# Float32r gate products, paired entry blocks and a split collection in a two-block transformer kernel

## The chip, the cores and the metric

The kernel runs on one NeuronCore of one Trainium2 chip. The metric is device time of one execution in microseconds (us). A core has TensorE (matrix products, PE in the profile, its weight loads PEld), VectorE (DVE), ScalarE (ACT), GpSimd (POOL) and SyncE (SP, which issues nearly all DMAs). Each engine works through its own queue in order; semaphores tie the queues together.

## The reference

One token block of 256 tokens with 1024 features goes through two transformer blocks, all in float32. The first has a mixer (retention and differential attention), then a product-key expert layer; the second has two layers of a gated short convolution or block attention, memory cross-attention and a SwiGLU. The expert layer is where most of the time lies:

```python
q = (hb @ w_query).reshape(t, PEER_HEADS, 2, PEER_HALF)
s = jnp.einsum('thpc,hpnc->thpn', q, sub_keys)
...
best, pos = lax.top_k(cand, PEER_TOPK)
experts = jnp.take_along_axis(cand_idx, pos, axis=-1)
gate = jax.nn.softmax(best, axis=-1)
act = jax.nn.gelu(jnp.einsum('thkd,td->thk', expert_u[experts], hb), approximate=False)
return jnp.einsum('thk,thkd->td', gate * act, expert_v[experts])
...
z = c_gate * u                     # short convolution: 3 taps over z, then
return (b_gate * conv) @ w_out     # gated by b_gate
```

Each token picks 16 experts in each of 8 heads, out of 128 x 128.

## The kernel before, in words

Activations lie transposed: features on the 128 partitions in 8 chunks, 256 tokens along the free axis. Precision comes from splitting: a weight tile `raw` (128x1024) is loaded by SP, rounded to float32r by ACT (`whi`, L118), and the rest is subtracted by DVE or POOL (`wlo`, L122, by `lo_plan`: "v" is DVE, "p" POOL). A block (`block`, L156; `mm3`, L134) is then 24 matmuls of 128x128 weights with 256 tokens: eight chunks each of whi·h_hi, wlo·h_hi and whi·h_lo. Its order is pass by pass, or, with `late`, chunk by chunk. There are three buffers of `raw` and `whi`, two of `wlo`. Large stages are dense rows of such blocks.

The expert layer (`peer`, L712) doesn't gather. It computes all 128x128 experts for all tokens: `slots` (128 partitions x 128 chunks x 256 tokens, 128 KB per partition) takes gelu(U·h2), is multiplied with a dense gate, and is multiplied with V.
- Entry: h2 is made chunk by chunk by DVE and ACT after a norm; 16 query blocks with `scores` behind each; `route` (DVE) picks the top 16 of each token, some steps after each block.
- U stage: 64 pairs of blocks (`peer_u`). From pair 16 on, gate groups stand between the blocks (`groups`). A group (`group`, L884) is four tokens: for each, `hot` builds two one-hot matrices on DVE (ohA: one comparison for two tokens; ohB: comparison times gate, one for each token) from `iota`, which lies in PSUM, and TensorE multiplies them in fp32, which gives the token's 128x128 gate. DVE multiplies it into the chunks that are done (L896, strided by tokens), ACT copies it to the chunks that are not (L898). For a finished token the later pairs are multiplied with the gate by DVE (L928).
- V stage: 128 chunks; ACT and DVE split `slots[:, c]` in two halves (`acth`, `actl`), twelve matmuls of 512 columns (`product`, L952). `mod_rest` loads and sums the last modulation weights beside the first of them. At the end `collect` copies, transposes and adds the output; the copies lie in the first slots.

Then comes the second block: `conv_mixer` (its `hook` loads the stored memory keys and values at block 1), `mem_attn`, `swiglu`, `moba`. A generator `filler` puts blocks of the memory's keys and values into waits, at places listed in `PLACES`; `track` sums squares for the next norm, adding on POOL (in the convolution's entry on DVE).

Order within each engine's queue is fixed at compile time by the framework's scheduler (program order as priority, by modelled times). Two readers of one PSUM bank of a tile are put one after the other.

Of the kernel before, what the change touches and what calls it, by code (L numbers as in the profile page):

```python
# [25 lines left out]
P = 128  # L26
T = 256
D = 1024
KC = 8
# [11 lines left out]
PLACES = {0: 1, 3: 1, 5: 2, 6: 1, 10: 1, 12: 1, 's': 2, 'h': 4, 'g': 10, 'n': 1, ('g', 0): 1, 'v': 4, ('d', 1): 1, ('o', 0): 3, ('o', 2): 1, ('o', 3): 1, ('o', 4): 1, ('o', 5): 4, ('o', 7): 10, ('c', 1): 1, ('c', 3): 1, ('c', 5): 1, 'ce': 1, 'm0': 1, 'mq0': 1, 'me0': 1, 'f0': 1, 'b': 2, 'bk': 1, 'bq': 1, ('mh0', 2): 1, ('bh', 0): 1, ('bh', 5): 1, ('bh', 7): 1}  # L41
# [15 lines left out]
CADD = 'vector'  # L57
MIXLO = 'v'
RETLO = 'v'
AHEAD = 3  # L60
# [11 lines left out]
class Build:  # L72
    def __init__(self, ctx, tc, io):
# [8 lines left out]
        self.adder = self.nc.gpsimd  # L82
# [51 lines left out]
    def mm3(self, out, pairs, first=True, last=True, late=False):  # L134
# [4 lines left out]
        if late:  # L139
            order.sort(key=lambda si: (si[1], si[0]))  # L140
# [15 lines left out]
    def block(self, out, src, x, cols=slice(None), lo=None, late=False, w=None):  # L156

        wh, wl = w or self.weight(src, lo)
        self.mm3(out, [(wh[:, k * P:(k + 1) * P], wl[:, k * P:(k + 1) * P],
                        x[0][:, k, cols], x[1][:, k, cols]) for k in range(KC)], late=late)  # L160

# [33 lines left out]
    def rstd(self, pool, sums, n, tag, shape=(P, T), bufs=1, a=None, y=None, tables=False, behind=None):  # L195
# [7 lines left out]
        log = nc.scalar.activation(y, a, AF.Ln)  # L203
# [79 lines left out]
    def constants(self):  # L283
# [6 lines left out]
        nc.vector.memset(self.ones, 1.0)  # L290
        self.x = c.tile([P, KC, T], F32, name="x")
# [10 lines left out]

    def mod_start(self, pool):
# [4 lines left out]
        warm = self.psum([P, P], "aux")  # L308
        for _ in range(WARM):
            nc.tensor.matmul(warm, self.ones, self.ones, start=True, stop=True)  # L310
# [136 lines left out]
    def mixer(self):  # L447
        nc, io, tc = self.nc, self.io, self.tc
        with ExitStack() as ctx:
# [7 lines left out]
            with ExitStack() as c1:  # L457
# [31 lines left out]
                for b in range(2):  # L489
                    for i in range(2):  # L490
                        self.block(gates[b][:, i], io["w_in_t"][12 + 2 * b + i], h, cols=X, late=b == i == 0)
                    self.at(("g", b))
# [158 lines left out]
            self.fill(20)  # L651

# [59 lines left out]
    def peer(self):  # L712
        nc, io = self.nc, self.io
        with ExitStack() as ctx:
            self.banks(ctx, "peer")
            big = self.pool(ctx, "slots")
            pool = self.pool(ctx, "peer")
            slots = big.tile([P, NCH, T], F32, name="slots")
            h = self.placed(pool, "h2h", 48), self.placed(pool, "h2l", 48)
# [16 lines left out]
            selT = gpool.tile([P, 3, T], F32, name="selT")  # L736
# [104 lines left out]
            def turn():  # L841

                for tt in range(2):
# [4 lines left out]
                    nc.scalar.copy(selT[:, :, cols], tr)  # L848
# [7 lines left out]
            ahead = query(0)  # L856
            for j in range(16):
                self.lo_plan = QPLAN[j // 4]
                q = ahead
                if j < 15:  # L860
                    ahead = query(j + 1)
# [6 lines left out]
            NG = T // TG  # L868

            def hot(g):  # L870


                for j in range(2):
                    A = gpool.tile([P, 2, P], F32, name="ohA", tag="ohA", bufs=HOT)
                    Bt = gpool.tile([P, 2, P], F32, name="ohB", tag="ohB", bufs=HOT)
                    t = g * TG + 2 * j
                    nc.vector.tensor_tensor(A, iota[:, None, :].to_broadcast([P, 2, P]),
                                            selT[:, 1, t:t + 2, None].to_broadcast([P, 2, P]), op=OP.is_equal)
                    for i in range(2):
# [72 lines left out]
            def product(c, th, a, b, w):  # L952
                tsl = slice(th * P, th * P + P)
                for s, (x, wt) in enumerate(((a, w[0]), (b, w[0]), (a, w[1]))):
                    for dh in range(2):
# [3 lines left out]
            def collect(th):  # L959

                tsl = slice(th * P, th * P + P)
                for q in range(4):
                    e = nc.scalar.copy if th or q % 2 else nc.vector.tensor_copy
                    e(ot[:, th, q * T:(q + 1) * T], acc[th][:, q // 2, q % 2 * T:q % 2 * T + T])
                for q in range(2):
                    tr = self.psum([P, 4, P])
                    for i in range(4):
                        k = 4 * q + i
                        nc.tensor.transpose(tr[:, i], ot[:, th, k * P:(k + 1) * P], self.ident)
                    for i in range(4):  # L970
                        k = 4 * q + i
                        nc.vector.scalar_tensor_tensor(self.x[:, k, tsl], tr[:, i], gate[:, k:k + 1],
                                                       self.x[:, k, tsl], op0=OP.mult, op1=OP.add)

            gate = self.mod[:, 40:48, 0]
            ot = slots[:, 0:8, :].rearrange("p (a c) t -> p a (c t)", a=2)
            for c in range(NCH - 2):
# [7 lines left out]
            ends = [(c, chunk(c)) for c in (NCH - 2, NCH - 1)]  # L985
# [637 lines left out]
```

## Time and profile before

| | us |
|---|---|
| median of 3 runs (lowest to highest) | 1889.74 (1888.1 to 1890.78) |
| profiled execution, of which span | 1882.41, 1880.6 |
| PE busy, of the span | 1833.2 (97%) |
| DVE / ACT / POOL busy | 1313.8 / 975.1 / 453.7 |

The span runs from the first to the last instruction of one profiled execution. A busy TensorE is not TensorE at its peak: matmuls are pipelined and each record holds its latency too, so the pace is read from the distance of starts. "Idle before" names what ended an engine's wait. The stages lie about so: mixer 0 to 287 us, queries to 347, U to 762, V to 1120, second block to the end.

### The profile page before, as it was taken

To read this page: it belongs to the slowest core of one execution; us is meant where nothing else is said; L and a number is where in the kernel's file an instruction comes from. 1 tells how busy PE (TensorE), PEld (TensorE's weight loads), DVE (VectorE), ACT (ScalarE), POOL (GpSimd) and SP (SyncE) were. 2 spreads that over 40 slices of the span, in tenths; PEclk is the share of its full clock that TensorE was granted. 3 is DMA by queue.
4 is the path that set the end of the run, shared out by engine and by line. 5 is a ranking of instruction groups with operands and counts; after the bars stand their busy time and mean duration, and the time that the engine had idled before them with its cause. 6 is when DMAs were issued, how large, how long until landed. Compare 5 with 4: busy or idle time off the path is not lost.

```text
span 1880.6 us, 34809 instructions
## 1 busy us (share of the span) xinstructions
PE 1833.2 (97%) x13562; PEld 1717.2 (91%) x13562; DVE 1313.8 (70%) x2592; ACT 975.1 (52%) x1533; POOL 453.7 (24%) x254
## 2 busy tenths in 40 slices
PE   8999999999999999999999998999999999999997
PEld 6796888999999999788888878999999999999997
DVE  7879875995566676865555568777765679766654
ACT  7746335445555444445545555465554645555543
POOL 0001105787766777100000004112000111110001
PEclk9999999999999999999999999999999999999999
DMA  8763444454444444755555555544555553445553
GB/s 298 254 217 105 142 129 156 170 189 169 150 160 154 157 157 157 247 191 195 195 191 193 196 192 184 191 169 148 200 193 196 190 180 124 169 136 190 187 184 124
DMA packets 99765, 335.13 MB, mean 178 GB/s; under 512 B 12400, under 2 KB 13456, under 8 KB 99216
## 3 DMA queue, kind: packets, MB, share of 16 engines
q1 hardware_dynamic: 98160, 330.68, 51.0%
q8 instruction: 106, 1.74, 0.4%
q10 hardware_dynamic: 1440, 2.23, 0.3%
q14 instruction: 59, 0.48, 0.1%
HBM read 329.59 MB, written 3.28 MB: 177 GB/s over the span
## 4 chain that ended last, share of the span: by engine, by line
PE 87%; DVE 6%; DMA 3%; ACT 3%; issue 1%; POOL 0%; SPq 0%; DVEq 0%; ACTq 0%; POOLq 0%
PE mm L144 54%; PE pair L956 17%; PE mm L179 4%; PE pair L893 3%; PE fill L179 2%; DVE wlo L122 2%; PE fill L144 1%; PE sc L144 1%; DMA mraw<-w_mod 1%; PE aux L144 1%; DMA raw<-w_mod 1%; ACT whi L118 1%; DMA raw<-peer_v 0%; PE sc L628 0%; PE sc L554 0%
## 5 line engine op out<-in xcount | busy, mean ns | idle before, releaser
L118 ACT CAST whi<-raw 128x1024 fp32r<-128x1024 f32 x564 | 591.9, 1051 | 558.3 <-PE mm L144 280.4
L122 DVE TENSOR_TENSOR wlo<-raw,whi 128x1024 fp32r<-128x1024 f32 x420 | 526.7, 1255 | 298.7 <-PE pair L956 131.6
L122 POOL TENSOR_TENSOR wlo<-raw,whi 128x1024 fp32r<-128x1024 f32 x144 | 344.7, 2395 | 131.6 <-PE mm L144 113.6
L144 PE MATMUL mm<-hh,whi 128*128 128x256 f32 (+1 forms) x1184 | 178.2, 287 | 5.9 <-DVE ct L1248 5.1
L144 PE MATMUL mm<-hl,whi 128*128 128x256 f32 (+1 forms) x1184 | 174.5, 284 | 2.1 <-DVE hl L261 1.2
L144 PE MATMUL mm<-hh,wlo 128*128 128x256 f32 (+1 forms) x1184 | 175.9, 285 | 0.0
L144 PE MATMUL mm<-h2h,whi 128*128 128x256 f32 x1152 | 168.2, 289 | 4.1 <-ACT h2h L260 4.0
L226 POOL TENSOR_TENSOR acc<-acc,accsq 128x256 f32<-128x256 f32 x42 | 42.1, 1004 | 523.1 <-ACT accsq L224 523.1
L144 PEld LDWEIGHTS mm<-hh,whi 128*128 128x128 f32 x1184 | 155.4, 190 | 10.9 <-issue 7.6
L956 PE MATMUL pair<-whi,actl 128*128 128x512 f32 x512 | 158.6, 391 | 2.4 <-DVE actl L949 2.3
L956 PE MATMUL pair<-whi,acth 128*128 128x512 f32 x512 | 158.3, 390 | 0.3 <-ACT acth L948 0.2
L956 PE MATMUL pair<-wlo,acth 128*128 128x512 f32 x512 | 157.8, 389 | 0.7 <-DVE wlo L122 0.7
L144 PEld LDWEIGHTS mm<-hl,whi 128*128 128x128 f32 x1184 | 153.5, 189 | 5.0 <-DVE hl L261 1.7
L144 PEld LDWEIGHTS mm<-hh,wlo 128*128 128x128 f32 x1184 | 154.6, 190 | 3.5 <-issue 1.5
L144 PE MATMUL mm<-h2h,wlo 128*128 128x256 f32 x1152 | 157.5, 279 | 0.0
L144 PE MATMUL mm<-h2l,whi 128*128 128x256 f32 x1152 | 157.1, 279 | 0.0
L144 PEld LDWEIGHTS mm<-h2h,whi 128*128 128x128 f32 x1152 | 147.4, 192 | 5.0 <-ACT h2h L260 4.8
L144 PEld LDWEIGHTS mm<-h2h,wlo 128*128 128x128 f32 x1152 | 144.6, 189 | 0.0
L144 PEld LDWEIGHTS mm<-h2l,whi 128*128 128x128 f32 x1152 | 144.0, 189 | 0.0
L956 PEld LDWEIGHTS pair<-whi,actl 128*128 128x128 f32 x512 | 95.4, 188 | 24.4 <-DVE actl L949 5.0
L956 PEld LDWEIGHTS pair<-wlo,acth 128*128 128x128 f32 x512 | 96.0, 188 | 21.3 <-DVE wlo L122 1.1
L956 PEld LDWEIGHTS pair<-whi,acth 128*128 128x128 f32 x512 | 95.5, 188 | 20.9 <-ACT acth L948 1.5
(407 smaller groups left out, 3062.7 us busy)
## 6 DMA issues: line engine op xcount, KB each, us to landing
raw<-peer_u SPq DMA_DIRECT2D x128, 512.0 KB, 3.5
raw<-peer_v SPq DMA_DIRECT2D x128, 512.0 KB, 3.5
raw<-ffn_gu SPq DMA_DIRECT2D x88, 512.0 KB, 4.3
raw<-ffn_dn SPq DMA_DIRECT2D x44, 512.0 KB, 3.9
raw<-w_mod SPq DMA_DIRECT2D x64, 256.0 KB, 3.8
raw<-conv_wi SPq DMA_DIRECT2D x24, 512.0 KB, 3.5
raw<-mem_wk SPq DMA_DIRECT2D x16, 512.0 KB, 4.5
mraw<-w_mod SPq DMA_DIRECT2D x16, 512.0 KB, 6.2
```

The costliest lines, as they stand in the source:

```text
L118: self.hi_copy = nc.scalar.copy(hi, raw)
L122: (nc.vector if plan == "v" else nc.gpsimd).tensor_sub(lo, raw, hi)
L144: self.matmul = nc.tensor.matmul(out, a, b, start=first and j == 0, stop=last and j == 3 * n - 1)
L179: self.matmul = nc.tensor.matmul(outs[i // 2][:, i % 2], a[:, k, :], b[:, w], start=k == 0 and s == 0 and i % 2 == 0, stop=k == 7 and s == ...
L226: self.adder.tensor_add(self.acc, self.acc, self.last)
L893: nc.tensor.matmul(o[:, 2 * j + i], A[:, i], Bt[:, i], start=True, stop=True)
L956: nc.tensor.matmul(acc[th][:, dh], x[:, tsl], wt[:, dh * 512:dh * 512 + 512], start=c == 0 and s == 0, stop=c == NCH - 1 and s == 2)
```

## The change

1. Gates. ohA and ohB become float32r. The transposed gate is split in a float32r part (`gate_hi`) and the ratio of the rest to it; ohB holds two matrices side by side, comparison times high part by DVE and that times the ratio by ACT. A token's product is one float32r matmul of 256 columns. The group's low halves are copied out by ACT, added by DVE; the product with the done chunks goes to POOL; the others get the sum by a DVE add. Three buffers of each instead of four, two ready ahead instead of three. The weights' low halves in this stage go by "ppvp" (one in four by DVE) instead of all by POOL.
2. Entry of the queries: `twin` runs two blocks in one order, chunk by chunk; products of ones stand in the wait before. The mixer's first two gate blocks and the convolution's first two blocks (in chunk pairs) go through `twin` as well.
3. End of V: only the last chunk is special; it goes by output halves, each collected behind the next one's product, into a tile `ot` of its own; the tiles of h2 are freed before V, and the pool of V takes their place. The convolution's first weights are loaded before that.
4. Second block: the keys' loads are spread over blocks from 3 on; the convolution's gate chain, the sums of squares, the subtractions of loaded keys and rope's product go from POOL to DVE (the gate chain's scaling to ACT); two fills move back; in `moba` the query features are made beside the values, and rope reads PSUM with tables that hold the norm. The norm's logarithm reads PSUM with a bias.

```diff
-PLACES = {... ('c', 1): 1, ('c', 3): 1, ('c', 5): 1, ...}
+PLACES = {... ('c', 5): 1, ...}
+WARM_N = 12
-GPLAN = "p"
-HOT = 4
+GPLAN = "ppvp"
+HOT = 3
-HOOK = 1
+HOOK = 3
-AHEAD = 3
+AHEAD = 2
...
-        self.adder = self.nc.gpsimd
+        self.adder = self.nc.vector
...
+    def twin(self, outs, ws, x, cols=slice(None), late=1, shared=False):
+        order = sorted(((k, s, i) for k in range(KC) for s in range(3) for i in range(2)),
+                       key=lambda z: (z[0] // late, z[1], z[2], z[0]))
+        for k, s, i in order:
+            wh, wl = ws[i]
+            xh, xl = x[0][:, k, cols], x[1][:, k, cols]
+            w = (wh, wl, wh)[s][:, k * P:(k + 1) * P]
+            self.matmul = self.nc.tensor.matmul(outs[i], w, (xh, xh, xl)[s], ...)
...
-        log = nc.scalar.activation(y, a, AF.Ln)
+        log = nc.scalar.activation(y, sums, AF.Ln, scale=1.0 / n, bias=self.eps)
...
+    def warm(self, n, bank="aux"):
+        o = self.psum([P, P], bank)
+        for _ in range(n):
+            self.nc.tensor.matmul(o, self.ones, self.ones, start=True, stop=True)
...
             self.tracked_norm(pool, "nr", urgent=True, y=self.r0, a=self.acc, tables=True)
             self.fill(20)
+            self.warm(WARM_N)
...
-                    nc.scalar.copy(selT[:, :, cols], tr)
+                    nc.scalar.copy(selT[:, :, cols], tr[:, 0:2])
+                    hi, ratio = gate_hi[:, cols], gate_ratio[:, cols]
+                    nc.scalar.copy(hi.bitcast(F32R), tr[:, 2])
+                    low, inv = stats[tt][:, 0:P], stats[tt][:, P:]
+                    nc.vector.tensor_sub(low, tr[:, 2], hi)
+                    nc.vector.tensor_scalar(inv, hi, 1e-36, None, op0=OP.max)
+                    nc.vector.reciprocal(inv, inv)
+                    nc.vector.tensor_mul(ratio, low, inv)
...
-            ahead = query(0)
+            os = [self.psum([P, T]) for _ in range(2)]
+            self.twin(os, [self.weight(io["w_query"][j]) for j in range(2)], h)
...
+                    for i in range(2):
+                        nc.vector.tensor_scalar(Bt[:, i, 0], iota, selT[:, 0, t + i:t + i + 1],
+                                                gate_hi[:, t + i:t + i + 1], op0=OP.is_equal, op1=OP.mult)
+                        nc.scalar.activation(Bt[:, i, 1], Bt[:, i, 0].bitcast(F32), AF.Copy,
+                                             scale=gate_ratio[:, t + i:t + i + 1])
...
-                    for i in range(2):
-                        nc.vector.tensor_scalar(Bt[:, i], iota, selT[:, 0, t + i:t + i + 1],
-                                                selT[:, 2, t + i:t + i + 1], op0=OP.is_equal, op1=OP.mult)
...
-                o = self.psum([P, TG, P], "pair")
+                o = self.psum([P, TG, 2, P], "pair")
...
+                lo = gpool.tile([P, TG, P], F32, name="glo", tag="glo", bufs=2)
+                nc.scalar.copy(lo, o[:, :, 1])
                 sl = slots[:, :, ts].rearrange("p c t -> p t c")
                 if done:
-                    nc.vector.tensor_mul(sl[:, :, :done], o[:, :, :done], sl[:, :, :done])
+                    nc.vector.tensor_add(lo[:, :, :done], o[:, :, 0, :done], lo[:, :, :done])
+                    nc.gpsimd.tensor_mul(sl[:, :, :done], lo[:, :, :done], sl[:, :, :done])
                 if done < NCH:
-                    nc.scalar.copy(sl[:, :, done:], o[:, :, done:])
+                    nc.vector.tensor_add(sl[:, :, done:], o[:, :, 0, done:], lo[:, :, done:])
...
             gctx.close()
+            hctx.close()
             pool = self.pool(ctx, "experts")
+            ot = pool.tile([P, 2, 1024], F32, name="ot")
...
-            ends = [(c, chunk(c)) for c in (NCH - 2, NCH - 1)]
-            for c, parts in ends:
-                product(c, 0, *parts)
-            product(ends[0][0], 1, *ends[0][1])
-            collect(0)
-            product(ends[1][0], 1, *ends[1][1])
-            collect(1)
+            parts = chunk(NCH - 1)
+            if "second" in self.parts:
+                self.conv_first = self.weight(io["conv_wi"][KC])
+            waiting = None
+            for dh in range(2):
+                for th in range(2):
+                    product(NCH - 1, th, *parts, halves=(dh,))
+                    if waiting:
+                        collect(*waiting)
+                    waiting = th, dh
+            collect(*waiting)
...
-                    nc.gpsimd.tensor_sub(lo, t, hi)
+                    nc.vector.tensor_sub(lo, t, hi)
+                    yield
...
-                cu = pool.tile([P, 2, T], F32, name="cu", tag="cu", bufs=2)
-                nc.vector.tensor_mul(cu, o, r[:, None, :].to_broadcast([P, 2, T]))
-                nc.gpsimd.tensor_mul(z, cu[:, 0], cu[:, 1])
-                nc.vector.tensor_scalar(y, z, cw[:, m, 2:3], None, op0=OP.mult)
+                nc.vector.tensor_mul(z, o[:, 0], r2)
+                nc.vector.tensor_mul(z, o[:, 1], z)
+                nc.scalar.activation(y, z, AF.Copy, scale=cw[:, m, 2:3])
...
-                nc.gpsimd.tensor_mul(y, y, r)
+                nc.vector.tensor_mul(y, y, r)
...
-                if m == HOOK:
-                    hook()
+                if m >= HOOK:
+                    for _ in range(2):
+                        next(hook, None)
...
+                if m == 0:
+                    self.twin([o[:, i] for i in range(2)], [self.conv_first, self.weight(io["conv_wi"][16])], h,
+                              late=2, shared=True)
...
+            def rope(out, o):
+                t = pool.tile([P, T], F32, name="roper", tag="roper", bufs=2)
+                nc.vector.stream_shuffle(t, o, [(i + 16) % 32 for i in range(32)])
+                nc.vector.tensor_mul(out, o, cosr)
+                nc.vector.tensor_mul(t, t, sinr)
+                nc.vector.tensor_add(out, out, t)
                 return out
```

## Rows read from the trace of the kernel before

**Rows 1.** The page, the chain that ended last: share of the span by engine.
```profile
PE 87%; DVE 6%; DMA 3%; ACT 3%; issue 1%; POOL 0%; SPq 0%; DVEq 0%; ACTq 0%; POOLq 0%
```

**Rows 2.** Busy sums by stretch: us, then PE, PEld, DVE, ACT, POOL, clock, DMA.
```profile
438.00:755.00 317.00, 317.00 (x2758) 317.00 (x2757) 196.37 (x494) 158.28 (x253) 224.82 (x95) 1.00 0.45 157
...
286.00:302.00 16.00, 11.74 (x66) 10.45 (x66) 9.68 (x23) 8.32 (x15) 4.34 (x3) 0.79 0.31 107
...
1119.50:1128.00 8.50, 5.44 (x31) 4.88 (x31) 7.85 (x23) 7.73 (x21) 0.00 (x0) 0.81 0.68 224
```

**Rows 3.** The chain that ended last, in order of time: start us, us, what.
```profile
347.84 90.34 PE mm L144 x767
...
544.95 5.46 PE mm L144 x48
...
551.30 2.83 PE mm L144 x24
...
555.02 5.46 PE mm L144 x48
...
1313.58 174.10 PE mm L144 x1536
...
1687.90 180.92 PE mm L144 x1536
```

**Rows 4.** Single instructions in order of time: start us, us, engine, line, operation, tiles.
```profile
278.82 0.73 POOL L226 TENSOR_TENSOR acc<-acc,accsq 128x256 f32<-128x256 f32 x1 [0.45 <-ACT accsq L224]
...
543.89 1.06 PE L893 MATMUL pair<-ohB,ohA 128*128 128x128 f32 x8
...
544.71 1.17 PE L144 MATMUL mm<-h2h,whi 128*128 128x256 f32 x8
...
549.01 0.31 ACT L927 ACTIVATE mm<-mm 128x176 f32<-128x176 f32 x1
...
734.62 1.27 DVE L896 TENSOR_TENSOR slots<-pair,slots 128x472 f32<-128x472 f32 x1
...
738.78 0.66 DVE L928 TENSOR_TENSOR slots<-mm,slots 128x480 f32<-128x480 f32 x1 [1.59 <-ACT mm L927]
...
756.45 2.97 DVE L949 TENSOR_TENSOR actl<-slots,acth 128x256 fp32r<-128x256 f32 x2 [0.54 <-ACT acth L948]
...
756.58 2.55 POOL L122 TENSOR_TENSOR wlo<-raw,whi 128x1024 fp32r<-128x1024 f32 x1 [1.28 <-ACT acth L948]
```

**Rows 5.** Groups of instructions by line, 438 to 755 us: count, busy us, mean ns.
```profile
L122 POOL TENSOR_TENSOR wlo<-raw,whi 128x1024 fp32r<-128x1024 f32 x95 | 227.1, 2391 | 94.0 <-PE mm L144 89.2 <-ACT slots L898 2.9 <-ACT whi L118 1.8
...
L118 ACT CAST whi<-raw 128x1024 fp32r<-128x1024 f32 x94 | 98.3, 1045 | 57.6 <-PE mm L144 51.8 <-DMA raw<-peer_u 2.9 <-POOL wlo L122 2.8
...
L896 DVE TENSOR_TENSOR slots<-pair,slots 128x128 f32<-128x128 f32 (+31 forms) x64 | 56.6, 884 | 5.2 <-PE pair L893 5.2
...
L898 ACT COPY slots<-pair 128x376 f32<-128x376 f32 (+46 forms) x63 | 33.2, 527 | 41.2 <-DVE slots L896 40.9
```

**Rows 6.** Groups of instructions by line and form, whole span.
```profile
L122 DVE TENSOR_TENSOR wlo<-raw,whi 128x1024 fp32r<-128x1024 f32 x420 | 526.7, 1255 | 298.7 <-PE pair L956 131.6 <-ACT whi L118 69.6 <-PE mm L144 43.0
...
L949 DVE TENSOR_TENSOR actl<-slots,acth 128x256 fp32r<-128x256 f32 x128 | 55.7, 436 | 4.0 <-ACT acth L948 3.8
```

**Rows 7.** Single instructions of TensorE where the queries begin.
```profile
292.16 5.85 PE L144 MATMUL mm<-h2h,whi 128*128 128x256 f32 x22 [4.05 <-ACT h2h L260]
...
302.08 0.60 PE L753 MATMUL pair<-slots 128*128 128x128 f32 x4
```

**Rows 8.** Single instructions of TensorE between the experts and the convolution.
```profile
1119.02 0.62 PE L956 MATMUL pair<-wlo,acth 128*128 128x512 f32 x2
...
1123.95 0.35 PE L144 MATMUL sc<-hh,whi 128*128 128x256 f32 x1 [2.07 <-ACT hh L274]
```

**Rows 9.** Waits of TensorE: for whom, us in total, times, longest us.
```profile
PE mm L144 <- DVE ct L1248: 5.1, 1, 5.1
...
PE sc L144 <- DVE wlo L122: 3.3, 1, 3.3
```

More of the change, by code (lines that the diff above doesn't have):

```diff
@@ L160, in block @@
                         x[0][:, k, cols], x[1][:, k, cols]) for k in range(KC)], late=late)
+    def twin(self, outs, ws, x, cols=slice(None), late=1, shared=False):
[5 more added lines that the diff above has]
+            w = (wh, wl, wh)[s][:, k * P:(k + 1) * P]
+            self.matmul = self.nc.tensor.matmul(outs[i], w, (xh, xh, xl)[s],
+                                                start=k == 0 and s == 0 and not (shared and i),
+                                                stop=k == KC - 1 and s == 2, skip_group_check=True)
     def natural(self, tag, srcs, toks, done, lo=None):
@@ L307, in mod_start @@
         nc.scalar.activation(self.sc, cc, AF.Silu)
-        warm = self.psum([P, P], "aux")
-        for _ in range(WARM):
-            nc.tensor.matmul(warm, self.ones, self.ones, start=True, stop=True)
+        self.warm(WARM)
         self.sc4 = pool.tile([P, KC, 4], F32R, name="sc4")
@@ L489, in mixer @@
                 for b in range(2):
-                    for i in range(2):
-                        self.block(gates[b][:, i], io["w_in_t"][12 + 2 * b + i], h, cols=X, late=b == i == 0)
+                    if b == 0:
+                        self.twin([gates[0][:, i] for i in range(2)], [self.weight(io["w_in_t"][12 + i]) for i in range(2)],
+                                  h, cols=X, shared=True)
+                    else:
+                        for i in range(2):
+                            self.block(gates[b][:, i], io["w_in_t"][12 + 2 * b + i], h, cols=X)
                     self.at(("g", b))
@@ L950, in chunk, with product, collect @@
                 return a, b, w
-            def product(c, th, a, b, w):
+            def product(c, th, a, b, w, halves=range(2)):
                 tsl = slice(th * P, th * P + P)
                 for s, (x, wt) in enumerate(((a, w[0]), (b, w[0]), (a, w[1]))):
-                    for dh in range(2):
+                    for dh in halves:
                         nc.tensor.matmul(acc[th][:, dh], x[:, tsl], wt[:, dh * 512:dh * 512 + 512],
                                          start=c == 0 and s == 0, stop=c == NCH - 1 and s == 2)
-            def collect(th):
+            def collect(th, dh):
                 tsl = slice(th * P, th * P + P)
[L962 to L973, printed above, removed]
+                for q in (2 * dh, 2 * dh + 1):
+                    nc.scalar.copy(ot[:, th, q * T:(q + 1) * T], acc[th][:, dh, q % 2 * T:q % 2 * T + T])
+                tr = self.psum([P, 4, P])
+                for i in range(4):
+                    k = 4 * dh + i
+                    nc.tensor.transpose(tr[:, i], ot[:, th, k * P:(k + 1) * P], self.ident)
+                for i in range(4):
+                    k = 4 * dh + i
+                    nc.vector.scalar_tensor_tensor(self.x[:, k, tsl], tr[:, i], gate[:, k:k + 1],
+                                                   self.x[:, k, tsl], op0=OP.mult, op1=OP.add)
             gate = self.mod[:, 40:48, 0]
-            ot = slots[:, 0:8, :].rearrange("p (a c) t -> p a (c t)", a=2)
-            for c in range(NCH - 2):
+            for c in range(NCH - 1):
                 if c == POS:
@@ L1349, in moba @@
             hk = self.gained(pool, self.x, G_KV)
+            nc.vector.tensor_scalar(self.gains[:, G_MIX + 1], self.gains[:, G_MIX + 1], 128.0 ** -0.5, None,
+                                    op0=OP.mult)
+            hq = [self.placed(pool, "hq" + c, 40) for c in "hl"]
+            cosr, sinr = (pool.tile([P, T], F32, name=n) for n in ("cosr", "sinr"))
             v = pool.tile([P, 2, 1024], F32, name="v")
@@ L1383, in moba @@
             kT = pool.tile([P, KC, T], F32, name="k")
-            hq = [self.placed(pool, "hq" + c, 32) for c in "hl"]
             def query(hd):
-                return plain(io["moba_wq"][hd], hq, 128.0 ** -0.5)
+                return plain(io["moba_wq"][hd], hq)
             def turned(t):
```

65 lines of the change are left out of this document (38 added, 27 removed).

## The prediction

> **What bounds the kernel now.** I read the chain that ended last first: TensorE's matmuls are 87% of it, so time is won by giving TensorE less to do or by closing its waits [rows 1]. Then I cut the span at the places the change touches and took the busy sums of each stretch [rows 2]. Between 438 and 755 us (matrix U with the gate products between its blocks) TensorE never idles, while DVE is busy 196 of 317 us, ACT 158 and POOL 225: all three have room, POOL least. The two changes of stage stand out by TensorE's granted clock: 0.79 from 286 to 302 us and 0.81 from 1119.5 to 1128 us, against 1.00 inside the stage.
>
> The chain in order of time gives the price of a block (24 matmuls of 128x256 fp32r) and of a gate group [rows 3]. Two places with 1536 matmuls each took 174.1 and 180.9 us, so one matmul goes at 113.3 or 117.8 ns; the first part of U (767 in 90.34 us) went at 117.8. Nothing in the rows says why a stage falls into one cadence or the other. From 544.95 to 555.02 us there are three blocks (5.46 + 2.83 us) and two groups: (10.07 - 8.29) / 2 = 0.89 us for a group. Its four fp32 products start at 543.89 and the next block at 544.71 [rows 4]: 0.82 us of products, the rest change-over.
>
> **The sum, part by part.** It is made against the profiled execution (1882.41 us, span 1880.6 and 1.8 around it).
>
> *Gates in float32r.* Each of the 256 tokens' products turns from one fp32 product of 128 columns into one fp32r product of 256 (high and low half of the gate side by side). A 256-column fp32r matmul is what a block is made of: 0.113 to 0.118 us, four of them 0.45 to 0.47. A group falls from 0.82 to 0.46 (without the change-over) or from 0.89 to 0.46 (with it): 64 groups give -23 to -27 us. I take -26, since both neighbours are then of one kind.
>
> *What pays for it.* The other engines get more per group, in 317 - 26 = 291 us [rows 2, 4, 5].
> ACT: 158.3 us, less the copies of L898 (33.2), plus 256 small scalings at about 0.28 (a 128x176 activation took 0.31) = 72, plus 64 copies of the low half, 512 wide, at about 0.55 (half of a 1024-wide cast, 1.045) = 35: 232 us, 80%.
> DVE: 196.4, less L896 (56.6), plus the adds of the done chunks (320 elements on average, contiguous; 480 took 0.66, so 0.45) = 29, plus the adds into the slots that are not done (192 elements with a stride; 472 strided took 1.27, so 0.55) = 35, plus 24 low halves of weights that the plan "ppvp" gives it, at 1.25 [rows 6] = 30: 234 us, 80%.
> POOL: 95 low halves less 24, 71 x 2.39 = 170, plus 64 products with the slots, 320 elements on average. POOL's 256-wide sum took 0.73 alone, so 0.9 contiguous; DVE's strided product costs about twice its contiguous one per element, so up to 1.8 here. That is 228 to 285 us, 78% to 98%. The last third, with 450 elements a product, is the tight part: per three blocks (about 9.1 us) 5.4 + 2 x 1.25 to 2 x 2.5 = 7.9 to 10.4. I take 1.6 in the mean (nearest to DVE's strided row, less its low end) and +5 us of waits for TensorE, bounds 0 and +20.
>
> What is queued behind: POOL's product waits for TensorE's group, ACT's copy and DVE's add; behind it stands a low half of a weight. Two of these are buffered, and a low half is written as soon as the pass of the block before has let its buffer go, so about two blocks stand between it and its reader; a delay of some 2 us is covered. If that cover is gone, every microsecond shows on TensorE.
>
> The trace shows one thing more against the change: at 756.45 us two DVE subtractions of 0.44 each took 2.97 us while a POOL subtraction ran [rows 4, 6]. [...] In rows: each of DVE's 24 new low halves has two SBUF inputs, and may wait out a POOL instruction (2.4) or hold one up (1.25): 24 x 1.25 = 30 us more on POOL at the worst, which makes 258 to 315 of 291. It is the reason for the +20, and for rival B.
>
> *Queries.* After the norm TensorE waits 4.05 us for the first chunk of h2, then runs 22 of two queries' 48 matmuls in 5.85 us while the eight chunks arrive (0.7 us each), and begins the first scores at 302.08, 4.1 us after these 22 [rows 7]. Chunk by chunk, only the last chunk's six matmuls (0.7) and a copy of some 0.4 stand behind the last arrival: -3 (bounds 0 and -4). The twelve products of ones lie in the 4.05 us wait: 24 passes of 128 columns, twice a group's eight (0.82), are 2.5 us, at half clock 5, so 1 us past it at the worst, which is in the bound. They would keep the clock up, and I count no more for it: the entry is then paced by DVE's chunks.
>
> *U to V.* The new pool lies where h2 lay, so the first halves of the slots can't be cast before U's last matmul: a cast and an activation of ACT, about 0.5 each by the 0.31 for 176 columns: +1 (0 to +3). The stage itself stays at 12 matmuls a chunk.
>
> *V to the convolution.* The last product starts at 1119.02 and runs 0.46, the next block starts at 1123.95 [rows 8]: 4.5 us with eight transposes. [...] Now output halves are collected behind the products of the next, the first weights of the convolution are loaded before, and the first two blocks go by pairs of chunks. Of the gap about 3 us go, of the slow stretch 1.6 to 2: -5 (bounds -1 and -7).
>
> *Convolution.* Two waits, 3.3 us for a low half of weights and 5.1 for the gated product [rows 9]. The loads of memory keys move from block 1 to blocks 3 and later, two fills move back, and the gate chain loses its POOL steps (0.73 us for 256 columns, more beside DVE) [rows 4]. Against that DVE gets the subtractions of the loaded keys and the sums of squares. I take half of the two waits, -4 (bounds 0 and -7).
>
> *Rest.* 42 POOL sums of squares and 12 subtractions go to DVE, and rope's product too; the logarithm reads PSUM one DVE step sooner, but the table load stands in the same place. Gates of the mixer go in pairs. Together -2 (bounds +4 and -5).
>
> *Cadence.* Two of the three long stretches in [rows 3] lie at 117.8, one at 113.3; where each falls anew is open. All of U and both feed-forward stages could shift by 4% of some 600 us, in part each: -2, bounds +9 and -11.
>
> Sum: -26 + 5 - 3 + 1 - 5 - 4 - 2 - 2 = -36: 1882.4 - 36 = 1846 for a profiled execution. The runs' median is 7.3 above the profiled one (1889.7), so I forecast **1853 us**.
>
> **Rivals.**
> B: the three helpers become the bound of the U stage. For it: POOL's sum of 258 to 315 of 291 with the lock, and three engines at 80% or more that wait in order for one another. Against it: the slack of two weight buffers, and that POOL in this stretch kept to 2.39 in every row. POOL at 1.6 to 1.8 a product plus 30 us of lock would end at 302 to 315 us: +11 to +24 instead of +5, so 1859 to 1872; I take 1868. [...]
> C: slower than before, by one mechanism: the strided product on POOL. Its price decides. Without lock POOL's stage is 170 + 64 X; the whole gain of 36 + 5 is gone when that reaches 291 + 41 = 332, X = 2.5 us, 7.9 ns per element, against 2.9 of the contiguous row. At X = 3, 362 us, and the time is 1889.7 - 41 + 71 = 1920. For it: steps of 1024 bytes on both sides, and no row of such a POOL instruction. Against it: DVE's strided row is only twice its contiguous one.
> D: the gain comes whole, the cadences fall low: -36 - 5 - 9 = -50, 1840.
>
> **How the numbers follow.** Forecast 0.58 (own range 1845 to 1862), B 0.20, D 0.12, C 0.07, and 0.03 for a result within 0.2% of before (3.8 us, what a measurement of this kernel can tell from no change), where B's end and the bounds of the small terms meet. The range reaches from D's lower side to B's upper, 1828 to 1880. Faster 0.89, same 0.03, slower 0.08.
>
> **What would show it.** In the changed profile a group of four products lies within 0.5 us between two blocks, and the U stage is about 20 us shorter. POOL is over 85% busy there; the mean of its new product says X directly. If TensorE's waits name POOL's or DVE's low halves there, B is right. The stretch of the queries ends 3 us sooner at a clock near 1.00; the gap before the convolution is under 2 us. Wrong would be: groups of over 0.6 us, a POOL product of over 2.5 us, or a U stage no shorter.

## The result, and the profile after

The changed kernel took 1865.36 us in the median of 4 runs (1858.93 to 1870.46) beside 1890.05 for the kernel before (4 runs, 1888.1 to 1890.78): a ratio of 0.9869, interval 0.9836 to 0.9902, or 24.7 us. Forecast were 36. The profiled execution took 1870.46 us, span 1868.7. First the page after: busy sums, then the chain's shares [rows 1].

```profile
PE 1818.3 (97%) x13330; PEld 1703.0 (91%) x13330; DVE 1358.7 (73%) x2760; ACT 1055.1 (56%) x1801; POOL 376.5 (20%) x201
...
PE 87%; DVE 5%; DMA 3%; ACT 3%; issue 1%; POOL 1%; SPq 0%; DVEq 0%; ACTq 0%; POOLq 0%
```

The chain is TensorE's as before. The stretches that answer to [rows 2], in the same columns:

```profile
438.00:751.00 313.00, 305.24 (x2574) 302.54 (x2573) 244.21 (x592) 238.34 (x516) 249.63 (x137) 0.99 0.46 162
440.00:520.00 80.00, 74.25 (x602) 73.31 (x601) 63.92 (x154) 57.58 (x129) 50.28 (x32) 0.96 0.43 152
284.00:302.00 18.00, 15.45 (x116) 14.96 (x114) 11.52 (x27) 9.06 (x18) 1.13 (x1) 0.91 0.38 135
1109.50:1118.00 8.50, 6.37 (x40) 6.18 (x41) 8.35 (x20) 8.29 (x21) 0.00 (x0) 0.80 0.52 170
...
640.00:740.00 100.00, 99.74 (x859) 98.53 (x858) 81.09 (x195) 78.42 (x172) 90.53 (x47) 1.00 0.47 168
```

The fourth of them doesn't lie where the row before does: it begins at the convolution's first matmul, 3.1 us after the last product. TensorE idles 7.8 us in the U stage, where it had idled nowhere, 5.8 of them in the stretch 440 to 520; in the last third, where POOL is busiest (90.5%), it lacks 0.26 us. The chain in order of time shows a group's price and the start of the groups [rows 3]; then one DVE and one POOL instruction in it:

```profile
449.62 0.24 DVE ohB L917
...
450.15 0.42 DVE ohA L921
450.57 0.21 DVE glo L939
450.78 0.88 DVE slots L942
451.66 3.22 DVE wlo L122
454.88 0.04 issue
454.93 3.78 PE mm L144 x16
...
505.52 0.47 PE pair L934 x4
505.99 5.65 PE mm L144 x48
511.64 0.47 PE pair L934 x4
```
```profile
451.50 3.37 DVE L122 TENSOR_TENSOR wlo<-raw,whi 128x1024 fp32r<-128x1024 f32 x1
...
451.45 2.33 POOL L122 TENSOR_TENSOR wlo<-raw,whi 128x1024 fp32r<-128x1024 f32 x1
```

A group lies between its neighbours in 0.47 us. At 451.66 TensorE waits for a weight's low half that DVE makes: DVE comes late to it, after five sets of group operands, and then needs 3.37 us instead of 1.255 [rows 6], which is POOL's 2.33 us and 1.04 more: it began 0.05 us behind POOL's and ended 1.09 us after it, as if it had stood until POOL's instruction was over. Below this is called the lock, as in the prediction. Behind the wait 16 matmuls take 3.78 us: twice the usual distance, at a granted clock of 0.50, which lasts 6.8 us from 453.7 on (the mean of 440 to 520 us is 0.96).

The new operations of the stage, by line: count, busy us, mean ns (438 to 751 us; answers to [rows 5]).

```profile
L122 POOL TENSOR_TENSOR wlo<-raw,whi 128x1024 fp32r<-128x1024 f32 x73 | 178.3, 2448 | 26.1 <-PE mm L144 15.3 <-ACT ohB L919 5.0 <-ACT whi L118 4.5
...
L919 ACT ACTIVATE ohB<-ohB,r 128x128 fp32r<-128x128 f32 x256 | 89.1, 398 | 26.1 <-DVE ohB L917 26.0
L940 POOL TENSOR_TENSOR slots<-glo,slots 128x128 f32<-128x128 f32 (+31 forms) x64 | 76.3, 1196 | 38.9 <-DVE glo L939 33.5 <-PE mm L144 4.8
```

TensorE's waits, as [rows 9] has them: for whom, us in total, times, longest.

```profile
PE mm L144 <- DVE wlo L122: 4.4, 2, 3.7
PE mm L144 <- ACT whi L118: 3.5, 3, 2.1
PE fill L191 <- DVE memv1l L1155: 2.7, 1, 2.7
PE mm L170 <- ACT h2h L272: 2.5, 1, 2.5
PE mm L144 <- DVE ct L1295: 2.5, 1, 2.5
...
PE mm L144 <- POOL wlo L122: 1.0, 1, 1.0
```

Of the convolution's 5.1 and 3.3 us, 2.5 and 0.6 are left. New are a wait of 2.7 between the feed-forwards, one of 1.0 for the third query's low half, and one of 2.1 for a weight of the convolution, six matmuls behind its start:

```profile
1109.51 0.71 PE L170 MATMUL sc<-hh,whi 128*128 128x256 f32 x4 [1.33 <-DMA memx<-memT]
1110.06 0.40 PE L170 MATMUL sc<-hh,wlo 128*128 128x256 f32 x2
1112.57 2.08 PE L144 MATMUL mm<-hh,whi 128*128 128x256 f32 x8 [2.11 <-ACT whi L118]
```
```profile
1108.28 3.30 ACT L286 ACTIVATE hh<-x,gains 128x256 fp32r<-128x256 f32 x8
1111.49 1.03 ACT L118 CAST whi<-raw 128x1024 fp32r<-128x1024 f32 x1
```

The two blocks that now run side by side need both weights at once. The first was loaded ahead; the cast of the second stands in ACT's queue behind all eight chunks of the input. So what the shorter gap gives is gone again: the convolution's 49th matmul starts 11.9 us after V's last product before (11.7 again) and 12.6 after (12.7 again).

Cut at the same matmuls, two profiled executions of each kernel (the second ones are experiments below) give this table of stages, in us:

| stage | before | again | after | again |
|---|---|---|---|---|
| start to h2's first matmul | 292.2 | 292.5 | 293.3 | 291.4 |
| queries | 55.4 | 54.6 | 55.0 | 53.6 |
| U, with the groups | 414.9 | 411.5 | 403.2 | 402.6 |
| V | 356.7 | 355.7 | 354.9 | 354.8 |
| last product to convolution | 4.7 | 4.7 | 3.1 | 3.1 |
| convolution, memory attention | 189.3 | 191.6 | 178.6 | 178.2 |
| gate and up matmuls, first feed-forward | 114.3 | 118.8 | 118.8 | 118.8 |
| from there to the second | 260.0 | 262.3 | 268.6 | 269.2 |

The second feed-forward and the tail are the same in all four. The convolution's gain and the loss two rows below are in part one thing: 48 fill matmuls, 5.4 us at 113.3 ns, moved from the one to the other. Together these two stages gain 4.3 in the mean, U 10.3, the rest 1.4: 16.0.

### The profile page after: what moved, and what is told of

Its sections match the earlier page's. It is cut to its first block, busy times and chain, and to the rows that moved or that the text cites. A ratio compares the mean times of both kernels' runs of the same rounds, so it can differ in the third digit from the quotient of the medians.

```text
span 1868.7 us, 34775 instructions
## 1 busy us (share of the span) xinstructions
PE 1818.3 (97%) x13330; PEld 1703.0 (91%) x13330; DVE 1358.7 (73%) x2760; ACT 1055.1 (56%) x1801; POOL 376.5 (20%) x201
## 4 chain that ended last, share of the span: by engine, by line
PE 87%; DVE 5%; DMA 3%; ACT 3%; issue 1%; POOL 1%; SPq 0%; DVEq 0%; ACTq 0%; POOLq 0%
PE mm L144 54%; PE pair L1002 17%; PE mm L191 4%; PE fill L191 2%; PE fill L144 1%; PE pair L934 1%; DVE wlo L122 1%; DMA mraw<-w_mod 1%; ACT whi L118 1%; PE aux L144 1%; PE mm L170 1%; PE sc L144 1%; DMA raw<-peer_v 1%; DMA raw<-conv_wi 0%; POOL wlo L122 0%
## 5 line engine op out<-in xcount | busy, mean ns | idle before, releaser
L122 DVE TENSOR_TENSOR wlo<-raw,whi 128x1024 fp32r<-128x1024 f32 x445 | 555.5, 1249 | 281.5 <-PE pair L1002 130.2
L122 POOL TENSOR_TENSOR wlo<-raw,whi 128x1024 fp32r<-128x1024 f32 x119 | 288.6, 2430 | 136.4 <-PE mm L170 86.5
L144 PE MATMUL mm<-h2h,whi 128*128 128x256 f32 x1136 | 159.1, 282 | 0.6 <-ACT whi L118 0.6
L917 DVE TENSOR_SCALAR ohB<-fill,selT,gatehi 128x128 fp32r<-128x128 f32 x256 | 95.9, 399 | 29.4 <-PE pair L934 29.2
```

The lines of the kernel that those rows point to most:

```text
L122: (nc.vector if plan == "v" else nc.gpsimd).tensor_sub(lo, raw, hi)
L144: self.matmul = nc.tensor.matmul(out, a, b, start=first and j == 0, stop=last and j == 3 * n - 1)
L917: nc.vector.tensor_scalar(Bt[:, i, 0], iota, selT[:, 0, t + i:t + i + 1], gate_hi[:, t + i:t + i + 1], op0=OP.is_equal, op1=OP.mult)
```

## The experiments

Each kernel is the changed one with the edit shown; medians are beside some 11 to 17 runs of the kernel before (medians 1888.2 to 1890.7).

**The changed kernel again.** No edit.

> The changed kernel once more, nothing edited. Theory (cadence falls anew in each execution): a stage's cadence of 113.3 or 117.8 ns a matmul is not fixed by the program. In the changed kernel's profile both feed-forward stages took 180.9 us; in this profile at least one stage of 1536 matmuls will read 174.1 (or a mean between), and the times will again spread over 5 us or more. Rival (the cadence is fixed by the program): both stages read 180.9 again, and the times lie within 3 us of one another. Against the kernel before both expect -20 to -28 us (24.7 measured).

1865.73 us (1863.84 to 1870.26), ratio 0.9876 [0.9840, 0.9911]. The first feed-forward took 118.8 us again and the waits stood at the same places with the same sizes, so they belong to the program. The expected faster stage did not come: here the rival held. The spread of 6 us came.

**The kernel before again.**

> The kernel before once more, nothing edited, for a profile of a typical execution (the first profile, at 1882.4 us, lies 8 us under the median). Theory (cadence): the 8 us lie in stages that ran at 113.3 ns a matmul in the first profile and run at 117.8 here; the feed-forward stage of 1536 matmuls that took 174.1 us reads 180.9, which is 6.8 of the 8. Rival (work between the stages is slower): that stage reads 174.1 again and the difference lies elsewhere.

1888.04 us, the profiled one 1886.56. The chain of this profile and the stage of [rows 3] it answers to:

```profile
347.40 86.94 PE mm L144 x767
...
1310.96 180.91 PE mm L144 x1536
```

The feed-forward of 174.10 us reads 180.91, and the first part of U, 90.34 in [rows 3], reads 86.94: the same instructions at the other cadence, one up, one down. So the cadence is not fixed by the program, and one profile of such a kernel is good to some 10 us only.

**Gates as before.**

```diff
-GPLAN = "ppvp"   HOT = 3   AHEAD = 2
+GPLAN = "p"      HOT = 4   AHEAD = 3
 # turn, hot, group: the fp32 versions of the kernel before
```

> The changed kernel with the gates as they were: one fp32 product of 128 columns a token, no split of the gate, no low-half copy, no add, no POOL product, all low halves of U's weights on POOL. Theory (what the profiles say): TensorE's groups cost 22.7 us more, the 11 us of waits and the 5 us of slower cadence that came with the change go; +7 to +14 us against the changed kernel, and TensorE has no wait over 0.7 us between 438 and 760 us. Rival 1 (the gates are worth nearly all of the measured 24.7, the waits came from something else in the stage): +20 to +25. Rival 2 (the gain lies in the other parts): under +4.

1876.11 us, ratio 0.9925 [0.9896, 0.9954]: +10.4 in the medians. No wait of TensorE over 0.7 us lies between 438 and 760. The gates are worth about what the U stage shows, 10 to 12 us: half or less of the 22 to 27 that they take off TensorE.

**All low halves of U on POOL.**

```diff
-GPLAN = "ppvp"
+GPLAN = "p"
```

> The changed kernel with every low half of U's weights on POOL again (one in four was on DVE). Theory (POOL would be full: 95 x 2.4 + 64 x 1.2 = 305 of 307 us): the wait of 3.9 us for DVE's low half at 451 us goes, but TensorE now waits for POOL's low halves in the last third of U, 5 to 15 us in all, so +2 to +12 us against the changed kernel. Rival (the lock between DVE's subtractions and POOL's is what costs, POOL alone keeps up): no such waits, -3 to -8 us.

1860.96 us, ratio 0.9852 [0.9821, 0.9884]: 4.8 less than the changed kernel, though the intervals overlap. Two stretches (columns as above) and the wait that is left:

```profile
440.00:520.00 80.00, 78.68 (x685) 78.22 (x684) 61.25 (x169) 65.51 (x148) 72.55 (x44) 1.00 0.52 171
...
640.00:740.00 100.00, 94.41 (x795) 91.60 (x794) 58.48 (x162) 71.72 (x151) 100.00 (x52) 1.00 0.47 155
```
```profile
PE mm L144 <- POOL wlo L122: 5.5, 7, 1.4
```

Both halves of the theory are there: the start loses its waits and its low clock (1.00 against 0.96), and POOL is full in the last third (100.00 of 100), where TensorE now lacks 5.6 us. But the first is worth more than the second costs.

**First group later, its operands made ahead.**

```diff
-ROUTE = 14, 15, 16
+ROUTE = 14, 15, 17
                 if cp == RT:
                     turn()
+                    ready.extend(next(parts) for _ in range(AHEAD))
```

> The changed kernel with the first gate group two blocks (5.6 us) later, and the operands of its first two pairs of tokens made as soon as the indices are turned. Theory (the 6.2 us of waits between 446 and 452 us come from DVE's queue: the split of the gate, five sets of operands and a low half at once): those waits shrink to under 2 us and the half clock after them (some 3 us) goes: -5 to -9 us against the changed kernel. Rival (DVE is as late two blocks further on, or the 64 groups in fewer blocks wait elsewhere): -2 to +3 us, with waits of the same size 5.6 us later.

1861.91 us, ratio 0.9848 [0.9817, 0.9879]: -3.8 in the medians. The waits of 6.2 us at the start fell to one of 2.0, and the clock from 440 to 520 rose to 1.00; waits for ACT's ohB of 1.7 us each at 566 and 682 came, against one of 1.4 before. Between theory and rival: about half of what the start costs comes back.

**A mix by place.**

```diff
-                self.lo_plan = UPLAN if cp < R1 else GPLAN   # GPLAN = "ppvp"
+                self.lo_plan = UPLAN if cp < 44 else GPLAN   # GPLAN = "pppvpp"
```

> The changed kernel with all low halves of U's weights on POOL up to pair of blocks 43, and from 44 on one in six on DVE (one in four from the start in the changed kernel). Theory (DVE's low halves hurt at the start, POOL's sum is over its time only in the last third, where the products are long): the waits at 446-452 go as when all were on POOL, and so do the 4.6 us of waits for POOL's low halves between 683 and 738: -5 to -9 us against the changed kernel, 0 to -4 against all on POOL. Rival (any DVE low half beside a POOL one costs more by the lock than the 2.5 us that it takes from POOL): not under all on POOL, with new waits for DVE's wlo in the last third.

1850.47 us (1846.94 to 1855.6), ratio 0.9824 [0.9787, 0.9860]: 15 less than the changed kernel in the medians, 9 by the ratios, and U is 389.4 us long in its profile, 396.7 and 392.0 in those of the two kernels below that keep the mix, against 402.6 to 403.2. So the mix is worth some 10 us; the rest of the 15 may be cadence. Of the waits at the start 1.07 and 0.60 us are left, of those for POOL in the last third 2.0. The six low halves on DVE took 2.13 us in the mean against 1.255 [rows 6], so POOL still costs them time, but six of them fit.

**Product with the slots on DVE**, all low halves on POOL.

```diff
-GPLAN = "ppvp"
+GPLAN = "p"
-                    nc.gpsimd.tensor_mul(sl[:, :, :done], lo[:, :, :done], sl[:, :, :done])
+                    nc.vector.tensor_mul(sl[:, :, :done], lo[:, :, :done], sl[:, :, :done])
```

> The changed kernel with all low halves of U's weights on POOL and the product with the slots on DVE instead. DVE in 445:740 would have 197 + some 72 = 270 of 295 us, POOL 226. Theory (POOL's queue was the bound of the last third with all low halves there, 100.0 of 100 us): the waits for POOL's low halves vanish; DVE's queue has room but is late at the groups, 0 to +4 against the run with all low halves on POOL (1861). Rival 1 (only POOL's load counted): -3 to -6 against it. Rival 2 (DVE becomes the bound): +5 or more, with waits for ohA and ohB.

1879.78 us (12 runs), ratio 0.9960 [0.9939, 0.9981]: +19 against the run with all low halves on POOL, rival 2. Its stage, the product's line, and TensorE's waits:

```profile
445.00:740.00 295.00, 281.32 (x2350) 273.71 (x2349) 268.32 (x589) 217.40 (x480) 225.75 (x88) 1.00 0.47 156
```
```profile
L940 DVE TENSOR_TENSOR slots<-glo,slots 128x136 f32<-128x136 f32 (+44 forms) x61 | 92.7, 1520 | 0.0
```
```profile
PE pair L934 <- ACT ohB L919: 9.6, 13, 1.3
PE pair L934 <- DVE ohA L921: 4.1, 8, 1.2
```

DVE at 268 of 295 us (91%) is late with every third group. The same product takes DVE 1520 ns, POOL 1196. Why shows in single rows: two DVE products of nearly one size took 1.15 and 1.92 us. The first began 0.22 us ahead of a POOL low half; the second began inside the next low half and outlasted it by 1.02. The two low halves took 5.61 together, 0.83 more than twice the 2.39 that is usual [rows 5].

```profile
683.88 1.15 DVE L940 TENSOR_TENSOR slots<-glo,slots 128x416 f32<-128x416 f32 x1
...
688.81 1.92 DVE L940 TENSOR_TENSOR slots<-glo,slots 128x424 f32<-128x424 f32 x1
...
684.10 5.61 POOL L122 TENSOR_TENSOR wlo<-raw,whi 128x1024 fp32r<-128x1024 f32 x2 [0.94 <-PE pair L934]
```

**Entry of the queries as before.**

```diff
-            self.warm(WARM_N)
...
-            self.twin(os, [self.weight(io["w_query"][j]) for j in range(2)], h)
+            ahead = query(0)
```

> The changed kernel with the entry of the queries as it was: the first two queries one after the other and no twelve products of ones in the wait. Theory (the profiles: 55.4 us from the first query matmul to U before, 53.6 to 55.0 after): the edit is worth 0.5 to 2 us, so +0.5 to +2 here, hardly to be told from nothing in the medians; in the profile the stretch from h2's first matmul to U reads 55 or more. Rival (it is worth its forecast): +3 us or more.

1860.87 us, ratio 0.9877 [0.9837, 0.9916]: nothing lost, perhaps something won. h2's first matmul waits 4.10 us here, 2.54 in the changed kernel, but there it is issued 0.7 us later after the norm's first sum (6.4 against 5.6 us): DVE's queue holds the second low half ahead of the last update of x. The queries took 54.5 us against 53.6 to 55.0. Products of ones before h2:

```profile
289.05 1.72 PE L321 MATMUL aux<-ones 128*128 128x128 f32 x14
293.31 0.79 PE L170 MATMUL mm<-h2h,whi 128*128 128x256 f32 x2 [2.54 <-ACT h2h L272]
293.91 0.63 PE L170 MATMUL mm<-h2h,wlo 128*128 128x256 f32 x2
```

These rows are of the changed kernel: the ones end 2.5 us before the first matmul, and the matmuls start 0.21 us apart, at a granted clock of 0.50 (293.3 to 296.6 us). That is not the rule, though. In the same kernel run again, behind the same ones and the same wait, they start 0.11 us apart:

```profile
291.38 0.51 PE L170 MATMUL mm<-h2h,whi 128*128 128x256 f32 x2 [2.54 <-ACT h2h L272]
...
298.08 0.71 PE L778 MATMUL pair<-slots 128*128 128x128 f32 x4
298.55 0.36 PE L144 MATMUL mm<-h2h,whi 128*128 128x256 f32 x1
299.95 1.20 PE L144 MATMUL mm<-h2h,wlo 128*128 128x256 f32 x8 [1.04 <-POOL wlo L122]
```
```profile
284.00:302.00 18.00, 14.11 (x111) 13.22 (x111) 9.96 (x24) 9.60 (x17) 4.47 (x2) 1.00 0.38 129
```

Of the ten profiles of kernels with the edit the granted clock from 284 to 302 us is 1.00 in seven and 0.91 in three, of which the changed kernel's first is one; in the four without the edit it is 0.81 (no run takes out the ones alone). And the first scores begin 6.7 us after h2's first matmul at the full clock, 8.1 at the lower one, against 9.0 to 9.9 without the edit. What takes this back stands in the last row: the third query waits for POOL's low half. POOL starts on it at 297.53 only, when TensorE's last matmuls of the first two queries let a buffer go: side by side the two hold both buffers to their end. From the first scores to U it is 46.9 us in all ten with the edit, 45.5 in all four without.

**End of V and convolution as before.**

```diff
-HOOK = 3
+HOOK = 1
+PLACES: ('c', 1): 1, ('c', 3): 1
 # product, collect, mem_load, mem_fill, conv_mixer: the versions of the kernel before
```

> The changed kernel with the end of V, the convolution and the loads of memory keys as they were (outputs collected in two halves inside the slots, no weight loaded ahead, first two blocks in order, POOL steps in the gate, fills back before the convolution's middle); the gates, the entry and the sums of squares stay changed. Theory (from the stages of the profiles: 4.7 us less in the gap with the conv's first blocks, most of the 8 us that the convolution stage loses and of the 8.6 us that the stage between the feed-forwards gains are the same 42 to 48 fill matmuls moved): +5 to +10 us. Rival 1 (the forecast: 5 for the gap and 4 for the waits): +9. Rival 2 (what is won at the gap is lost again to the moved fills and the wait of 2.9 us for a value's low half): 0 to +3.

1864.54 us, ratio 0.9884 [0.9846, 0.9921]: rival 2. By the stages: the gap 4.7 instead of 3.1, the convolution 187.8 instead of 178.4 (5.4 of it moved fills), the stage between the feed-forwards 258.5 instead of 268.9. The edit wins 5.6 us up to the first feed-forward and loses 5.0 behind it. The 5.6 come from the convolution's later waits: its 49th matmul starts 11.9 us after V's last product here, 12.6 in the changed kernel.

**Fills back, on top of the mix by place.**

```diff
-PLACES = {... ('c', 5): 1, ...}
+PLACES = {... ('c', 1): 1, ('c', 3): 1, ('c', 5): 1, ...}
```

> The fastest so far (all low halves on POOL up to pair 43, then one in six on DVE) with the two fills back before blocks 1 and 3 of the convolution. Theory (moved to the place between the feed-forwards, the 48 fill matmuls bring a wait of 2.9 us for a value's low half; in the convolution they lay over waits): -2 to -4 us against it, no wait of 2.9 us there. Rival (they bring the wait with them into the convolution): 0.

1852.23 us (1841.69 to 1855.51), ratio 0.9817 [0.9782, 0.9853]: the same as without. In the profile the wait of 2.7 us is gone, the stage between the feed-forwards is 7.2 shorter (260.2 against 267.4) and the convolution 4.5 longer; the 2.7 that this leaves don't show in the medians. What hides such amounts is seen in U, whose code is the same in both (the mix alone, then with the fills back):

```profile
500.00:600.00 100.00, 100.00 (x881) 99.82 (x880) 70.43 (x198) 80.98 (x181) 98.71 (x56) 1.00 0.51 170
```
```profile
500.00:600.00 100.00, 100.00 (x851) 100.00 (x851) 68.91 (x192) 79.37 (x174) 95.65 (x55) 1.00 0.50 165
```

TensorE is busy 100.00 of 100 us at clock 1.00 in both, and does 881 matmuls in one, 851 in the other.

**Entry undone as well.** The edit of the entry shown above, on this kernel.

> The same as the one before it, with the entry of the queries undone as well (two queries one after the other, no products of ones). Theory (the second low half put into DVE's queue delays the last update of x by 0.75 us, and the chunk by chunk order gains about 1 in the queries): within 1.5 us of the one before it. Rival (the products of ones keep the clock up and are worth 2 or more): +2 to +4 us.

1853.50 us, ratio 0.9838 [0.9807, 0.9869]: 1.3 more, within what was expected; in the medians the entry's edit has no effect that can be measured.

**The small edits undone.**

```diff
-        self.adder = self.nc.vector
+        self.adder = self.nc.gpsimd
-        log = nc.scalar.activation(y, sums, AF.Ln, scale=1.0 / n, bias=self.eps)
+        log = nc.scalar.activation(y, a, AF.Ln)
 # mixer's first gates, rope and the second queries: the versions of the kernel before
```

> The changed kernel with the small edits undone: the sums of squares added on POOL again, the logarithm fed by DVE's step instead of PSUM, the mixer's first pair of gates as two blocks in order, rope and the second queries as they were. Gates, entry, end of V and convolution stay changed. Theory (undoing the end of V and the convolution costs nothing in the medians and undoing the gates 10 us of 25, so the rest carries the remainder; by the profiles the convolution and the stage between the feed-forwards hold 7 us that the undone convolution doesn't give back): +5 to +10 us, with longer waits in the convolution and between the feed-forwards. Rival (the forecast of 2; the remainder is cadence): 0 to +3.

1867.99 us, ratio 0.9915 [0.9883, 0.9947]: +2.3 in the medians, +0.0039 in the ratio (some 7 us, with an uncertainty as large). The waits for value low halves between the feed-forwards rose from 2.7 to 4.3. Not decided between 2 and 7.

## Why the prediction was right, and where its sizes were off

The sign held and the time lies in the range, but 3 us above the likeliest case's own range (1845 to 1862), and the gain is 25 us instead of 36. It is nearer to rival B's 1868, and one of B's signs came (TensorE's waits in U name DVE's low half), but not its mechanism: over the stage the three helpers are busy 76 to 80%, and they are late mainly at its start. Of the other signs the group within 0.5 us came (0.47); U is 12 us shorter, not 20, POOL is busy 80% there, not over 85%, and the gap before the convolution is 3.1 us, not under 2.

*Gates, -26.* Right. A group is 0.47 us (forecast 0.46): 64 groups give 22 us less by the products alone (0.82 before), 27 with the change-over (0.89).

*Waits, +5 (0 to +20).* The term that was mis-sized: TensorE's waits in the stage, read from the distance of its starts, sum to some 11 us; half clock (0.50 for 6.8 us, 5.6 of them behind the longest wait, so 2.8 lost) and cadence come on top. The sum was made over the whole stage and looked for trouble in the last third, on POOL. There TensorE loses 0.26 us. The waits came at the first groups, where DVE splits the gates, makes five sets of operands and has one of four low halves queued behind them; the lock makes that low half last 3.37 us, and the clock falls to 0.50 before TensorE goes on. The runs with low halves on POOL, with a later start and with the mix by place each took most of this away, and each was faster.

*Loads of the helpers.* Estimated 232 (ACT), 234 (DVE), 228 to 285 (POOL); 238, 244 and 250 in 438 to 751. The POOL product (the prediction's X) was put at 1.6 us and is 1.20; C needed 2.5. DVE, whose strided row gave the 1.6, was the slower engine for it where it had the product (1.52). Of the 30 us of lock feared for POOL 73 x 0.057 = 4 came (2448 against 2391), and on DVE 24 x 0.4 = 10 (1653 ns in the mean against 1255). In the stage DVE's low halves, with both inputs in SBUF, took 1.20 to 3.37 us and POOL's 2.33 to 3.39, while DVE's 256 operations for ohB, with iota in PSUM, kept to 0.35 to 0.45. B's cause, helpers that bind, held only in experiments: where POOL has all low halves, for the last 100 us, and where DVE has the product.

*Queries, -3.* Its mechanism held and its sum left out what pays for it. Up to the first scores 2.3 to 3.2 us are won at the full clock, and in most profiles that clock holds; where it falls, 1.4 of this is lost. Two terms were put at nothing: the second weight's low half goes into DVE's queue ahead of x's last update (0.7 us), and the third query waits 1.0 us for POOL's low half (1.4 us longer from the first scores to U). The queries took 0.7 us less in the mean of the two profiles, and nothing shows in the medians. (The ones' 24 passes are three times a group's eight, not twice; their 2.5 us is right.) *U to V, +1:* there, 1.1 us.

*V to the convolution, -5.* Failed. The gap gave 1.6 of its 3 us, and TensorE then waits 2.1 for the second weight, whose cast the sum left out; the first two blocks end some 0.8 us later after V's last product than before. No run shows the 1.6 to 2 us that the sum takes from a slow stretch: where the convolution begins the granted clock was 0.50 for 3.4 us before and for 3.4 us in the changed kernel. *Convolution, -4.* Better than counted: 5.6 up to the first feed-forward with that loss in it, so some 6 from the waits and the gate chain. What failed is that "two fills move back" was priced at nothing. The experiment with the end of V and the convolution undone shows 5.0 us lost behind the first feed-forward; in their new place the fills wait 2.7 us for a value's low half, and the rest of the 5.0 is not explained.

*Rest, -2:* between 2 and 7, undecided. *Cadence, -2 (+9 to -11):* not the same in each execution (the first feed-forward took 114.3 and 118.8 us in the two of the kernel before), as the bounds took it; in the profile it went against the change, 4.5 us in that stage alone (118.8 against 114.3).

What stays open: the medians differ by 23 to 25 us, the profiled executions by 16. And the parts undone one at a time give 10.4 - 4.9 - 1.2 + 2.3 = 6.6 us in the medians, where the whole gives 23. By the ratios, each taken beside runs of the kernel before, the same four are 10, 1, 2 and 8: 21 of 24 us. Each of these is uncertain by some 7 us, so neither sum settles whether parts help one another.

## What to carry to other kernels

Add up helpers' loads by stretch, not by stage: where a new phase starts, its first operands, its set-up and the ordinary work stand in one queue, and that is where a helper with 20% to spare was late here (DVE, busy 244 of 313 us). Which engine gets a share of the work can change with the place: this kernel gained 10 to 15 us by leaving DVE alone while the phase starts and easing POOL only where the products are long. Work that is moved out of a stage has to be priced in the stage that it goes to. And a shorter gap is worth only what the next wait leaves of it: here the third query's low half and the convolution's second weight took back what two edits had won.

## What the hardware showed that was not expected

One stage with the same instructions, no waits and clock 1.00 ran at 113.3 ns a matmul in one execution and 117.8 in another, and kept its pace throughout (178 or 179 matmuls in every 20 us at the one, 172 or 173 at the other, in the changed kernel). That is 6.8 us on 1536 matmuls, more than most single edits here; which pace a stage takes no row explains.

The clock at one place isn't fixed by the program either. Behind the same products of ones and a wait of 2.5 to 2.8 us it stayed at 1.00 in seven profiles and fell in three (0.91 over 18 us; 0.50 for 3.4 us in the changed kernel's first).

A DVE subtraction that started 0.05 us behind POOL's lasted 3.37 us: POOL's whole 2.33 and 1.04 more, where 1.255 is usual. The price shows in means too: DVE's low half took 1255 ns over the whole kernel before, where POOL is busy a quarter of the time, 1653 in the U stage of the changed kernel (POOL 80%), and 2126 in the last third of the mix by place (POOL 97%).
